# The first 8 MB load of a row-sum kernel, cut into four loads of 32 partitions that are four apart

## The chip, the cores and the metric

The kernel runs on one core of one Trainium2 chip. The metric is the device time of one execution in microseconds (us). Of the core's engines this kernel uses VectorE (DVE) and ScalarE (ACT) for arithmetic, SyncE (SP) to issue all transfers, and the core's 16 DMA engines to carry them out. GpSimd (POOL) only sets a few constants; TensorE does nothing.

## What is computed

```python
def setup_inputs():
    batch, seq, dim = 32, 512, 1024
    return {"x": np.random.randn(batch, seq, dim).astype(np.float32)}

def reference(x):
    relu_x = np.maximum(x, 0)
    return np.sum(relu_x, axis=-1).astype(np.float32)
```

There are 32 x 512 = 16,384 rows of 1,024 floats. Each is clamped at zero and summed. 67.1 MB are read, 64 KB are written.

## The kernel before

**Tiling.** The rows are split into two halves in name only: the first 2,048 rows (`xf`) and the rest (`xv`). In each, partition p holds consecutive rows, so that what one load brings to one partition is contiguous in memory. A full block is 16 rows for each of 128 partitions: 64 KB a partition, 8 MB in all. Three such buffers in on-chip memory (`io0`, `io1`, `io2`; `NBUF = 3`) are used in turn.

**Loop.** For each of seven blocks (`j`), `load` (L97) issues one transfer of 8 MB from SP into a buffer. From the fourth block on, it waits before that until DVE has read the buffer's former contents (`freed`). Each load has a semaphore of its own, which counts up by 16 as the transfer completes; the first computing instruction of the block waits for 16. In the first blocks ACT clamps the whole block in place (`clamp`, L115) and DVE then sums it along the rows (`total`, L123), in one, later two pieces a block (`TWO`). In the sixth and seventh blocks some rows are done by ACT alone (`act_row`, clamp and sum in one instruction) or by DVE alone (`dve_row`).

**Tail.** The last 8 MB come in loads that get smaller: 8 rows a partition, 4 rows, 2 rows and 280 elements (1,164 KB), 1 row and 260 elements (642 KB), and two pieces of 240 and 244 elements, so that little work is left after the last byte. ACT and DVE share these rows one by one. Three stores bring the sums out; the last waits for the very last sum.

**Order.** The order on every engine is the order in which the code names the instructions. All loads and stores are issued by SP on one queue, so they are carried out one behind the other. Nothing separates the engines at the start: `open_without_barrier` (L238) takes the drains and semaphore waits out of the opening block and moves SP's first `EARLY` loads (here one, L24, L48) from the body into the opening block, ahead of SP's first instruction there, so that they are issued before SP branches to the body. On SP the order is thus: the load of `io0`, the branch, the loads of `io1` and `io2`, then the loads that wait for DVE, the tail, the stores.

Of the kernel before, what the change touches and what calls it, by code (L numbers as in the profile page):

```python
# [9 lines left out]
ROWS = 16  # L10
NBUF = 3
# [9 lines left out]
START_PIECE, END_PIECE = 280, 260  # L21
PIECES = [240, 244]

EARLY = 1  # L24


def kernel(tc: tile.TileContext, x: bass.AP, out: bass.AP):
    nc = tc.nc
    sems = Semaphores(tc)

    tc.close()
    tc.compile()
    nc.cur_bb = nc.bb_map[tc.start_bb_name]
    body = nc.cur_bb.bb.instructions
    ends = list(body)
    body.clear()
    n_stores = relu_sum(nc, sems, x, out)
    body.extend(ends)


    nc.cur_bb = nc.bb_map[tc.start_bb_name + "_end"]
    nc.cur_bb.bb.instructions.clear()
    nums = sorted(s.num for s in (*sems.loads, sems.act, sems.dve))
    cleared = range(nums[0], nums[-1] + 1)
    assert len(cleared) == len(nums)
    nc.sync.sem_clear(cleared)
    nc.sync.wait_ge(sems.stored, 16 * n_stores).then_inc(sems.stored, -16 * n_stores)
    open_without_barrier(tc, EARLY)  # L48

# [10 lines left out]
def relu_sum(nc, sems: Semaphores, x: bass.AP, out: bass.AP):  # L60
    x_flat = x.flatten_outer_dims()
    N, D = x_flat.shape
    NT = N // P
    NB = len(TWO)
    assert N == P * NT == P * ROWS * (NB + 1)
    assert sum(TAIL) == ROWS - 4 and START_PIECE + END_PIECE + sum(PIECES) == D

    bufs = [nc.alloc_sbuf_tensor(f"io{i}", [P, ROWS, D], F32) for i in range(NBUF)]
    res = nc.alloc_sbuf_tensor("res", [P, NT], F32)

    extra = len(PIECES) + 1
    parts = [
        nc.alloc_sbuf_tensor(f"piece{i}", [P, w + extra * (i + 1 == len(PIECES))], F32)
        for i, w in enumerate(PIECES)
    ]


    N1 = P * ROWS
    xf = x_flat[:N1].rearrange("(p m) d -> p m d", p=P)
    xv = x_flat[N1:].rearrange("(p m) d -> p m d", p=P)  # L80
    o_flat = out.rearrange("b s -> (b s)")
    of = o_flat[:N1].rearrange("(p m) -> p m", p=P)
    ov = o_flat[N1:].rearrange("(p m) -> p m", p=P)

    def rows(m, n):
        if m < ROWS:
            return xf[:, m : m + n, :]
        return xv[:, m - ROWS : m - ROWS + n, :]

    def sums(m, n):  # L90
        if m < ROWS:
            return of[:, m : m + n], res[:, m : m + n]
        return ov[:, m - ROWS : m - ROWS + n], res[:, m : m + n]

    n_load = n_act = n_dve = n_store = 0

    def load(dst, src, after=None):  # L97
        nonlocal n_load
        dma = nc.sync.dma_start(out=dst, in_=src)  # L99
        if after:  # L100
            dma.wait_op(sems.dve, after[1], "sem-ge")
        dma.then_inc(sems.loads[n_load], 16)
        n_load += 1
        return sems.loads[n_load - 1]

    def store(m, n, act, dve):
        nonlocal n_store
        dst, src = sums(m, n)
        nc.sync.wait_ge(sems.act, act)
        nc.sync.dma_start(out=dst, in_=src).wait_op(sems.dve, dve, "sem-ge").then_inc(  # L110
            sems.stored, 16
        )
        n_store += 1

    def clamp(ap, loaded):  # L115
        nonlocal n_act
        i = nc.scalar.activation(out=ap, in_=ap, func=RELU)  # L117
        if loaded is not None:
            i.wait_op(loaded, 16, "sem-ge")
        i.then_inc(sems.act, 1)  # L120
        n_act += 1

    def total(ap, m, n):  # L123
        nonlocal n_dve
        nc.vector.tensor_reduce(  # L125
            out=res[:, m : m + n], in_=ap, axis=mybir.AxisListType.X, op=ADD
        ).wait_op(sems.act, n_act, "sem-ge").then_inc(sems.dve, 1)
        n_dve += 1

    def act_row(ap, accum_out, loaded):  # L130
        nonlocal n_act
        i = nc.scalar.activation(out=ap, in_=ap, func=RELU, accum_out=accum_out)  # L132
        if loaded is not None:
            i.wait_op(loaded, 16, "sem-ge")
        i.then_inc(sems.act, 1)
        n_act += 1

    def dve_row(ap, accum_out, loaded):
        nonlocal n_dve
        i = nc.vector.tensor_scalar(  # L140
            out=ap,
            in0=ap,
            scalar1=0.0,
            scalar2=None,
            op0=MAX,
            op1=ADD,
            accum_out=accum_out,
        )
        if loaded is not None:
            i.wait_op(loaded, 16, "sem-ge")  # L150
        i.then_inc(sems.dve, 1)
        n_dve += 1

    freed = []
    m = 0
    for j in range(NB):
        buf = bufs[j % NBUF]
        loaded = load(buf[:, :, :], rows(m, ROWS), j >= NBUF and freed[j - NBUF])
        c = 0
        act_waits = dve_waits = loaded  # L160
        for n in TWO[j]:
            clamp(buf[:, c : c + n, :], act_waits)
            total(buf[:, c : c + n, :], m + c, n)
            act_waits = None
            c += n
        for _ in range(ACT[j]):
            act_row(buf[:, c, :], res[:, m + c : m + c + 1], act_waits)
            act_waits = None
            c += 1
        for _ in range(DVE[j]):  # L170
            dve_row(buf[:, c, :], res[:, m + c : m + c + 1], dve_waits)
            dve_waits = None
            c += 1
        assert c == ROWS
        freed.append((n_act, n_dve))
        m += ROWS


    buf = bufs[NB % NBUF]
    c = 0  # L180
    for n in TAIL:
        loaded = load(
            buf[:, c : c + n, :], rows(m, n), None if c else freed[NB - NBUF]
        )
        for i in range(n):
            if i % 2 == 0 or (n == 8 and i == 7):
                act_row(buf[:, c, :], res[:, m : m + 1], loaded if i == 0 else None)
            else:
                dve_row(buf[:, c, :], res[:, m : m + 1], loaded if i == 1 else None)
            c += 1  # L190
            m += 1

    flat = buf[:, :, :].rearrange("p c d -> p (c d)")
    src = rows(m, 4).rearrange("p c d -> p (c d)")
    at = c * D
    split = 2 * D
    b = split + START_PIECE
    end = split + D - END_PIECE
    last, w = parts[-1], PIECES[-1]
    others = [last[:, w + i : w + i + 1] for i in range(extra)]  # L200
    loaded = load(flat[:, at : at + b], src[:, :b])
    act_row(buf[:, c, :], res[:, m : m + 1], loaded)
    sums_act = n_act
    dve_row(buf[:, c + 1, :], res[:, m + 1 : m + 2], loaded)
    sums_dve = n_dve
    dve_row(flat[:, at + split : at + b], others[0], None)
    loaded = load(flat[:, at + end : at + 4 * D], src[:, end:])
    act_row(buf[:, c + 3, :], res[:, m + 3 : m + 4], loaded)
    dve_row(flat[:, at + end : at + 3 * D], others[1], loaded)
    arrived = []  # L210
    for part, n in zip(parts, PIECES):
        arrived.append(load(part[:, :n], src[:, b : b + n]))
        b += n
    assert b == end

    store(0, ROWS, *freed[0])
    store(ROWS, NT - ROWS - 2, sums_act, sums_dve)

    for i in range(len(PIECES) - 1):
        dve_row(parts[i][:, :], others[2 + i], arrived[i])
    nc.vector.wait_ge(arrived[-1], 16)
    nc.vector.tensor_scalar(  # L224
        out=last[:, :],
        in0=last[:, :],
        scalar1=0.0,
        scalar2=None,
        op0=MAX,
        op1=ADD,  # L230
        accum_out=res[:, NT - 2 : NT - 1],
    ).wait_op(sems.dve, n_dve, "sem-ge").then_inc(sems.dve, 1)
    n_dve += 1
    store(NT - 2, 2, n_act, n_dve)
    return n_store


def open_without_barrier(tc: tile.TileContext, n_loads: int):  # L238

    SP = mybir.EngineType.SP
    blocks = tc.nc.main_func.blocks
    opening = blocks[0].instructions
    body = next(b for b in blocks if b.name == tc.start_bb_name).instructions
    for i in list(opening):
        if isinstance(i, (mybir.InstDrain, mybir.InstEventSemaphore)):
            opening.remove(i)
    loads = [i for i in body if i.engine == SP][:n_loads]
    for i in loads:  # L250
        assert isinstance(i, mybir.InstDMACopy)
        body.remove(i)
    at = next(n for n, i in enumerate(opening) if i.engine == SP)
    opening[at:at] = loads
# [30 lines left out]
```

## Time and profile before

| | |
|---|---|
| time, median of 3 runs | 161.14 us (161.03 to 161.29) |
| span of the profiled execution, first to last instruction | 159.62 us |
| busy: DVE | 117.6 us (74%) |
| busy: ACT | 104.2 us (65%) |
| DMA | 67.18 MB in 2,304 packets, mean 421 GB/s over the span |
| first load, issue to landing | 21.8 us |
| issue of the first load on SP | 0.38 us, from 0.00 |
| issues of the second and third load | 0.42 and 0.43 us, from 0.43 and 0.90 |

The profile is of one execution. It gives that execution's span; its device time was not taken beside it, so the median of the runs stands for it: 1.52 us more than the span, which lie before the first and after the last instruction.

Line numbers (L99) are lines of the kernel. "SPq" is SP's DMA queue as the issuer. A DMA packet here is one contiguous piece for one partition: 64 KB in the large loads. Its bytes are counted in the stretch of time in which the packet starts, so that GB/s over a short stretch is a count of packets that start in it. Arrows show who ended a wait.

### The profile page before, as it was taken

The numbers are of one execution on the slowest core, as the hardware profiler recorded it, in microseconds if no ns is written. First come the engines' busy times: TensorE is split into PE (matmuls) and PEld (weight loads), VectorE is DVE, ScalarE is ACT, GpSimd is POOL, SyncE is SP. The second block draws the span as 40 slices with busy tenths as digits, with TensorE's granted clock in tenths as the row PEclk, the third lists the DMA queues.
The fourth block names the chain that finished last, engine by engine and source line by source line (L and its number), as shares of the span: only waits on it lengthen the run. The fifth ranks groups of instructions, "written<-read, shape, count | busy, mean of one in ns | idle before, by whom it ended". The sixth has DMA issues, their size and how long they took to land.

```text
span 159.6 us, 120 instructions
## 1 busy us (share of the span) xinstructions
DVE 117.6 (74%) x43; ACT 104.2 (65%) x50; POOL 0.2 (0%) x4
## 2 busy tenths in 40 slices
DVE  0000000009999499994999999999999999999986
ACT  3000059990699708996099951999329993499995
POOL 0000000000000000000000000000000000000000
DMA  7996996996997999979979969969969969798993
GB/s 279 509 526 263 526 526 263 526 509 279 526 476 312 526 394 394 526 345 443 526 328 460 526 263 526 526 263 526 509 279 526 493 296 526 337 452 382 418 412 119
DMA packets 2304, 67.18 MB, mean 421 GB/s; under 512 B 640, under 2 KB 896, under 8 KB 1024
## 3 DMA queue, kind: packets, MB, share of 16 engines
q1 hardware_dynamic: 2304, 67.18, 98.0%
HBM read 67.11 MB, written 0.07 MB: 421 GB/s over the span
## 4 chain that ended last, share of the span: by engine, by line
DMA 43%; DVE 34%; ACT 17%; another core or an unknown queue 3%; SPq 1%; issue 0%
DMA io<-in_x_dram 43%; DVE res L125 32%; ACT io L117 17%; DVE io L140 1%; SPq L99 1%; DVE piece L224 0%; DVE piece L140 0%
## 5 line engine op out<-in xcount | busy, mean ns | idle before, releaser
L125 DVE TENSOR_REDUCE res<-io 128x8 f32<-128x8192 f32 (+2 forms) x9 | 101.1, 11287 | 40.0 <-ACT io L117 40.0
L117 ACT ACTIVATE io<-io 128x8192 f32<-128x8192 f32 (+2 forms) x9 | 81.7, 9110 | 47.7 <-DMA io<-in_x_dram 47.7
L132 ACT ACTIVATE io<-io 128x1024 f32<-128x1024 f32 x20 | 20.9, 1045 | 6.0 <-DMA io<-in_x_dram 6.0
L140 DVE TENSOR_SCALAR_CACHE_REDUCE io<-io 128x1024 f32<-128x1024 f32 (+2 forms) x15 | 15.8, 1110 | 0.5 <-DMA io<-in_x_dram 0.4
L132 ACT ACTIVATION_READ_ACCUMULATOR io<-io 128x1 f32 x20 | 3.8, 188 | 0.0
L117 ACT ACT_TABLE_LOAD x1 | 1.3, 1283 | 0.1
L140 DVE DVE_READ_ACCUMULATOR io<-io 128x1 f32 x15 | 1.2, 82 | 0.0
L224 DVE TENSOR_SCALAR_CACHE_REDUCE piece<-piece 128x247 f32<-128x247 f32 x1 | 0.4, 410 | 0.0
L140 DVE TENSOR_SCALAR_CACHE_REDUCE piece<-piece 128x240 f32<-128x240 f32 x1 | 0.4, 397 | 0.0
L269 POOL MEMSET const-bfloat16-1.0<- 128x1 bf16 x1 | 0.1, 101 | 0.0
L269 POOL MEMSET const-uint8-127<- 128x1 uint8 x1 | 0.1, 101 | 0.0
L269 POOL MEMSET const-float32-0.0<- 128x1 f32 x1 | 0.1, 98 | 0.2 <-issue 0.2
L269 POOL MEMSET const-float32-1.0<- 128x1 f32 x1 | 0.1, 98 | 0.0
L224 DVE DVE_READ_ACCUMULATOR piece<-piece 128x1 f32 x1 | 0.1, 83 | 0.0
L140 DVE DVE_READ_ACCUMULATOR piece<-piece 128x1 f32 x1 | 0.1, 82 | 0.0
## 6 DMA issues: line engine op xcount, KB each, us to landing
io<-in_x_dram SPq DMA_DIRECT2D x1, 4096.0 KB, 21.6
io<-in_x_dram SPq DMA_DIRECT2D x1, 2048.0 KB, 26.1
io<-in_x_dram SPq DMA_DIRECT2D x1, 1164.0 KB, 28.4
io<-in_x_dram SPq DMA_DIRECT2D x1, 642.0 KB, 29.5
piece<-in_x_dram SPq DMA_DIRECT2D x1, 122.0 KB, 29.2
piece<-in_x_dram SPq DMA_DIRECT2D x1, 120.0 KB, 29.4
io<-in_x_dram SPq DMA_DIRECT2D x7, 26.9
out_dram<-res SPq DMA_DIRECT2D x1, 55.0 KB, 1.6
```

Of the source, the lines that this page charges most:

```text
L99: dma = nc.sync.dma_start(out=dst, in_=src)
L117: i = nc.scalar.activation(out=ap, in_=ap, func=RELU)
L125: nc.vector.tensor_reduce(out=res[:, m : m + n], in_=ap, axis=mybir.AxisListType.X, op=ADD).wait_op(sems.act, n_act, "sem-ge").then_inc(se ...
L132: i = nc.scalar.activation(out=ap, in_=ap, func=RELU, accum_out=accum_out)
L140: i = nc.vector.tensor_scalar(out=ap, in0=ap, scalar1=0.0, scalar2=None, op0=MAX, op1=ADD, accum_out=accum_out,)
L224: nc.vector.tensor_scalar(out=last[:, :], in0=last[:, :], scalar1=0.0, scalar2=None, op0=MAX, op1=ADD, accum_out=res[:, NT - 2 : NT - 1],) ...
L269: nc = _bacc.Bacc("TRN2", target_bir_lowering=False, num_devices=1)
```

## The change

The first block's load is cut into four. Load q takes partitions q, q + 4, q + 8, ..., 32 of them, each with its whole 64 KB. The four are issued from SP one behind the other, count up the same semaphore by 16 each, and the first clamp waits for 64. `EARLY` is now 4, so all four go into the opening block, ahead of the branch. `load` returns the count to wait for beside the semaphore, and the helpers wait for that. On SP the order is now: four loads into `io0`, the branch, the loads of `io1` and `io2`, and all else as it was. No other engine's instructions change.

```diff
-EARLY = 1
+EARLY = 4
...
-        return sems.loads[n_load - 1]
+        return sems.loads[n_load - 1], 16
+
+    def load_in_parts(dst, src):
+        nonlocal n_load
+        for q in range(EARLY):
+            dma = nc.sync.dma_start(out=dst[q::EARLY], in_=src[q::EARLY])
+            dma.then_inc(sems.loads[n_load], 16)
+        n_load += 1
+        return sems.loads[n_load - 1], 16 * EARLY
...
-            i.wait_op(loaded, 16, "sem-ge")
+            i.wait_op(*loaded, "sem-ge")
...
-        loaded = load(buf[:, :, :], rows(m, ROWS), j >= NBUF and freed[j - NBUF])
+        if j == 0:
+            loaded = load_in_parts(buf[:, :, :], rows(m, ROWS))
+        else:
+            loaded = load(buf[:, :, :], rows(m, ROWS), j >= NBUF and freed[j - NBUF])
...
-    nc.vector.wait_ge(arrived[-1], 16)
+    nc.vector.wait_ge(*arrived[-1])
```

More of the change, by code (lines that the diff above doesn't have):

```diff
@@ L133, in act_row @@
         if loaded is not None:
-            i.wait_op(loaded, 16, "sem-ge")
+            i.wait_op(*loaded, "sem-ge")
         i.then_inc(sems.act, 1)
@@ L149, in dve_row @@
         if loaded is not None:
-            i.wait_op(loaded, 16, "sem-ge")
+            i.wait_op(*loaded, "sem-ge")
         i.then_inc(sems.dve, 1)
```

## The prediction

> **What bounds the kernel now.** I read the shares first. The page's DMA rows (mean busy share of the 16 engines in 40 slices, then the queue's total) and the span:
>
> ```profile
> span 159.6 us, 120 instructions
> ...
> DMA  7996996996997999979979969969969969798993
> ...
> q1 hardware_dynamic: 2304, 67.18, 98.0%
> ```
>
> The digits jump because a 64 KB packet is booked in the slice where it starts; the last line counts: the DMA engines were moving packets for 98% of the span. No compute engine comes near (DVE 74%, ACT 65%). Next, the order of time on ACT, whose clamps (L117) each wait for one whole 8 MB load:
>
> ```profile
> 21.87 13.86 ACT L117 ACTIVATE io<-io 128x16384 f32<-128x16384 f32 x1 [20.47 <-DMA io<-in_x_dram]
> 41.19 13.86 ACT L117 ACTIVATE io<-io 128x16384 f32<-128x16384 f32 x1 [5.46 <-DMA io<-in_x_dram]
> 60.55 13.86 ACT L117 ACTIVATE io<-io 128x16384 f32<-128x16384 f32 x1 [5.50 <-DMA io<-in_x_dram]
> 79.90 13.95 ACT L117 ACTIVATE io<-io 128x8192 f32<-128x8192 f32 x2 [5.50 <-DMA io<-in_x_dram]
> ```
>
> Columns: start, duration, instruction, idle before it and who ended that. Loads land 19.32 to 19.36 us apart. A load is 128 rows of 64 KB, 8 rows for each of 16 engines, so a row takes 19.35/8 = 2.42 us. The first load lands at 21.87, 2.5 us more than 19.35: that start-up is paid once, and since the queue never runs dry, a change of it shifts the end one for one. The queue's cover: io0 is issued again at 53.00, the queue has work until 60.5. At the end the chain of waits goes through a landing and then DVE alone:
>
> ```profile
> 126.91 28.43 DMA io<-in_x_dram
> 155.34 0.02 issue
> 155.37 2.02 DVE io L140 x6
> ```
>
> DVE had been idle 0.43 us before 155.37. Its earlier reduces start when ACT's clamps end, so they move with the landings too.
>
> Then the start-up in short windows (first column the window, second its width, last column GB/s; GB/s by width by 1/65,536 gives how many packets start there):
>
> ```profile
> 1.00:1.25 0.25, 0.00 (x0) 0.25 (x1) 0.00 (x0) 1.00 8.52 2884
> 1.25:1.50 0.25, 0.00 (x0) 0.15 (x1) 0.00 (x0) 1.00 1.47 524
> 1.50:1.75 0.25, 0.00 (x0) 0.00 (x0) 0.00 (x0) 1.00 1.41 524
> 1.75:2.00 0.25, 0.00 (x0) 0.00 (x0) 0.00 (x0) 1.00 0.62 262
> ...
> 3.95:4.20 0.25, 0.00 (x0) 0.00 (x0) 0.00 (x0) 1.00 3.02 1311
> 4.20:4.45 0.25, 0.00 (x0) 0.00 (x0) 0.00 (x0) 1.00 5.44 2359
> 4.45:4.70 0.25, 0.00 (x0) 0.00 (x0) 0.00 (x0) 1.00 1.21 524
> ```
>
> 11, 2, 2 and 1 engines start their first row in the first four; 5, 9 and 2 turn to their second row in the last three. Narrower windows put the first two turns between 3.90 and 4.00 and the last between 4.55 and 4.60: a spread of 0.6 us, with first rows that take about 3 us instead of 2.42. It stays: 130 us later (134.50 to 135.25) the counts by quarter microsecond are 6, 8 and 2. A load lands when its last engine is done, so the engine that turned at 4.58 sets every landing. What counts is that time.
>
> **The change, part by part.** Durations are from the execution whose span is 159.62 us; the median of the runs is 161.14, 1.52 more, which lies around the span and which nothing here touches. The sum is a difference, taken off both.
>
> *Removed and added.* One issue of 128 rows becomes four of 32, rows q, q+4, q+8 and so on. Same bytes, same 128 rows of 64 KB, all waited for together (count 64 instead of 16 on the same clamp). Four issues stand ahead of SP's branch where one did.
>
> *A, the last engine's turn.* If the spread of 0.62 comes from 128 rows being described to the engines in one go, a quarter of the rows leaves a quarter of it: a gain of 0.75 x 0.62 = 0.46. Against that stands the last store (L110): also 128 rows, but of 8 bytes, into an empty queue. Issued at 158.19, all its rows and completions pass between about 159.01 and 159.21, so its engines start at most about 0.15 us apart; three quarters of that is 0.11. The first load is nearer in size and place, the store cleaner; I take the middle, 0.29.
>
> *B, the first byte.* The first issue occupies SP for 0.38 us, the first packet starts at 1.01; the last store needs 0.82 from issue to first packet. If the issue shrinks with the rows, 0.75 x 0.38 = 0.29 is gained; if a 32-row issue costs what the later back-to-back ones do (0.42 to 0.46), 0.06 is lost. I take 0.13.
>
> *C, three more completions for each engine.* The last store is 9 packets on each engine (8 rows, 1 completion) in 0.2 us: at most 0.023 each, 0.07 for three. I take 0.03.
>
> *D, what is moved behind three more issues.* On SP the loads of io1 and io2 go out at about 1.8 and 2.2 instead of 0.43 and 0.90. They are needed when the first load's rows run out, at about 20.9: 18 us of cover. The re-issue of io0 at 53.00 waits for DVE (L125), not for SP. POOL's four sets and ACT's table load (over at 1.40) depend on none of it. Without that cover it would be 3 x 0.44 = 1.3 us. Cost 0.
>
> Sum: 0.29 + 0.13 - 0.03 = 0.39 gained, span 159.23, median 161.14 - 0.39 = 160.75. By the ends: 161.14 - 0.46 - 0.29 = 160.39, and 161.14 - 0.11 + 0.06 + 0.07 = 161.16.
>
> The row on splitting: loads queued behind each other land 19.35 us apart with no gap of their own. [...] No row here shows a 32-row load.
>
> **The rivals.**
>
> *R1, the spread is the memory's.* Each engine still opens with one 64 KB row, and its 3 us may come from the memory's first answers, whatever number of rows was described. For it: the last store's small spread, and that of the 16 engines the one starting last (after 1.75) isn't the one turning last, as 2.42 after 1.8 is below 4.58. Then A = B = 0, C 0.03: 161.17, no change that can be told. The change then does not do what it sets out to do.
>
> *R2, the run of issues holds the engines back (slower).* In the trace the engines' first starts, 1.0 to 1.8, fall in and just behind the time in which SP issues io1 and io2 (0.43 to 1.33). If each issue that follows takes the descriptions' path away from engines still to be started, the spread of 0.62 is 0.31 for each of two; now five follow, until about 2.6. Three more cost 0.93, C 0.03, against B's 0.13: 161.97. It decides as soon as the last engine turns after 4.58. Against it: 11 of 16 engines start by 1.25, with the third issue still under way.
>
> *R3, the rows are dealt badly (slower).* If 32 rows reach only 8 engines, or meet in pairs, the first load takes twice its 19.35: 161.14 + 19.35 = 180.5, hidden by nothing, since the queue is full. Against it: 32 is a multiple of 16, two rows for each; nothing in the trace speaks for it.
>
> **How the numbers follow.** My forecast, an earlier last engine, has 0.64; R1 0.13; R2 0.19; R3 0.04. A change under 0.2% (0.32 us) is about what a measurement of this kernel can't tell from none. The forecast's own range is 160.39 to 161.16; of its 0.64 I put 0.54 below 160.82 and 0.10 above. Faster 0.54; same 0.10 + 0.13 = 0.23; slower 0.19 + 0.04 = 0.23. The predicted time is 160.75. The range of 8 in 10 goes from 160.3, just past the best ends, up to 161.9, to the foot of R2's price; R3 and the upper part of R2 are left out.
>
> **What would show it.** A: the last engine's turn to its second row before 4.45, the counts by quarter microsecond bunched closer, and the same closeness 130 us on. B: first packets before 0.95. C: landings of the later loads still 19.35 apart. D: io1 issued near 1.8 with no dent in the DMA shares at 21. The first clamp should start near 21.5 instead of 21.87, and every later clamp as much earlier. R1 shows as an unchanged spread, R2 as first turns later than 4.6, R3 as a first clamp near 41. I am wrong if first rows keep their 3 us whatever the number described at once, or if DVE's 0.43 us of idle time before 155.37 closes, which would mean that something other than the landings has come to bind.

## The result and the profile after

| | before | changed |
|---|---|---|
| median of 8 runs each (lowest to highest) | 161.06 us (160.84 to 161.29) | 161.39 us (161.30 to 161.58) |
| ratio to before | | 1.002, 95% interval 1.0011 to 1.0029 |
| span of the profiled execution | 159.62 us | 160.00 us |
| first issue on SP | 0.38 us | 0.55 us |
| first clamp | 21.87 us | 22.22 us |

The change made the kernel 0.33 us slower, or 0.18 to 0.47 by the interval; the forecast was 0.39 us faster. The chain of waits of the changed kernel (start, duration, what) says where it begins:

```profile
0.00 0.55 SPq L109
0.55 0.06 issue
0.60 0.58 SPq L109
...
1.86 0.59 SPq L109
2.45 0.04 issue
2.49 39.06 DMA io<-in_x_dram
```

A 32-row part takes SP 0.55 to 0.59 us where the 128-row load took 0.38, and all four end at 2.45 instead of the 1.8 expected. The start-up in short windows (GB/s in the last column, to be read as a count of packets that start, as in the prediction):

```profile
1.00:1.25 0.25, 0.00 (x0) 0.25 (x1) 0.00 (x0) 1.00 0.00 0
1.25:1.50 0.25, 0.00 (x0) 0.15 (x1) 0.00 (x0) 1.00 6.40 2097
1.50:1.75 0.25, 0.00 (x0) 0.00 (x0) 0.00 (x0) 1.00 3.92 1311
...
4.20:4.45 0.25, 0.00 (x0) 0.00 (x0) 0.00 (x0) 1.00 1.82 786
4.45:4.70 0.25, 0.00 (x0) 0.00 (x0) 0.00 (x0) 1.00 3.63 1573
4.70:4.95 0.25, 0.00 (x0) 0.00 (x0) 0.00 (x0) 1.00 4.23 1835
```

Between 1.00 and 1.25, where 11 engines had started, none does; a narrower window puts the first starts between 1.30 and 1.35 instead of 1.01. The turns to the second row lie in the last three windows (3, 6 and 7 engines). The earliest falls between 4.30 and 4.35 instead of just before 4.00, the latest between 4.90 and 4.95 instead of 4.55 to 4.60. Both ends have moved by about 0.35; the spread is 0.6 as before. From there on the time only follows. ACT in order of time:

```profile
22.22 13.86 ACT L125 ACTIVATE io<-io 128x16384 f32<-128x16384 f32 x1 [20.83 <-DMA io<-in_x_dram]
41.58 13.86 ACT L125 ACTIVATE io<-io 128x16384 f32<-128x16384 f32 x1 [5.50 <-DMA io<-in_x_dram]
60.92 13.86 ACT L125 ACTIVATE io<-io 128x16384 f32<-128x16384 f32 x1 [5.49 <-DMA io<-in_x_dram]
```

The loads still land 19.34 to 19.36 us apart, each 0.35 to 0.4 later than before. Nothing is won back in the 140 us that follow, and nothing more is lost: from the first clamp to the end of the span it is 137.76 us before and 137.77 after.

So the question was which property of the new loads makes the first issue and the first packet late. Three theories: S, the step of four partitions from one row of a load to the next; N, the small number of rows in a load; Q, the run of further issues right behind the first one (the prediction's R2).

### The profile page after: what moved, and what is told of

It reads as the page before. It is cut to its first block, busy times and chain, and to the rows that moved or that the text cites. A ratio compares the mean times of both kernels' runs of the same rounds, so it can differ in the third digit from the quotient of the medians.

```text
span 160.0 us, 123 instructions
## 1 busy us (share of the span) xinstructions
DVE 117.6 (74%) x43; ACT 104.2 (65%) x50; POOL 0.2 (0%) x4
## 4 chain that ended last, share of the span: by engine, by line
DMA 42%; DVE 34%; ACT 17%; another core or an unknown queue 3%; SPq 2%; issue 0%
DMA io<-in_x_dram 42%; DVE res L133 32%; ACT io L125 17%; SPq L109 1%; DVE io L148 1%; SPq L99 0%; DVE piece L235 0%; DVE piece L148 0%
```

## The experiments

Unless a diff says otherwise, each kernel is the changed one with the edit shown. Times stand beside runs of the kernel before on the same chip: 161.03 us in the first set of four, 161.09 in the second, 161.11 in the third, 161.08 for the last run.

### Four loads of 32 neighbouring partitions

```diff
-            dma = nc.sync.dma_start(out=dst[q::EARLY], in_=src[q::EARLY])
+            near = slice(P // EARLY * q, P // EARLY * (q + 1))
+            dma = nc.sync.dma_start(out=dst[near], in_=src[near])
```

> The first 8 MB in four loads of 32 neighbouring partitions instead of partitions four apart; the output stays the reference's. Reference points: before, the first issue takes 0.38 us, the first packet starts at 1.01, the first clamp at 21.87; in the changed kernel 0.55, 1.33 and 22.22. Theory S (the step of four partitions makes a load's issue and start longer): issue near 0.38, first packet near 1.01. Theory N (few rows in a load do): 0.55 and 1.33 as in the change. Theory Q (the run of issues behind the first load holds its start back): 1.33 as in the change, the issue itself no judge. [...]

Measured: 181.90 us, ratio 1.1294 (1.1277 to 1.1310). SP's first issue, from its order of time, and the first window of starts:

```profile
0.00 0.38 SPq L110 DMA_DIRECT2D io<-in_x_dram  x1
```

```profile
0.95:1.20 0.25, 0.00 (x0) 0.25 (x1) 0.00 (x0) 1.00 11.05 2359
```

The issue takes 0.38 us again and nine engines have started by 1.20. The same window of the kernel before has ten:

```profile
0.95:1.20 0.25, 0.00 (x0) 0.25 (x1) 0.00 (x0) 1.00 7.75 2621
```

N falls: 32 rows cost SP no more than 128. The large loss is of another kind, as ACT shows:

```profile
43.02 13.86 ACT L126 ACTIVATE io<-io 128x16384 f32<-128x16384 f32 x1 [41.62 <-DMA io<-in_x_dram]
```

The first 8 MB need twice the time, which is the price that the prediction's R3 names. How the rows run, in windows of this kernel (the number before GB/s is the time of the packets that start in the window, as a share of 16 engines' time):

```profile
1.00:1.25 0.25, 0.00 (x0) 0.25 (x1) 0.00 (x0) 1.00 12.29 2621
1.25:2.00 0.75, 0.00 (x0) 0.15 (x1) 0.00 (x0) 1.00 2.23 524
2.00:4.00 2.00, 0.00 (x0) 0.00 (x0) 0.00 (x0) 1.00 0.00 0
...
8.00:12.00 4.00, 0.00 (x0) 0.00 (x0) 0.00 (x0) 1.00 1.28 262
```

Ten and six rows start by 2.00, so sixteen are under way, as in the kernel before, and not eight. But the 16 rows that start between 8 and 12 take 5.12 us each (1.28 x 16 x 4.00 us, shared by 16), where a row takes 2.42 in the kernel before and in the changed one. In these runs, then, 32 neighbours ran at about half rate and 32 partitions four apart at full rate; why, no view here shows.

### Two loads of 64 partitions, two apart

```diff
-EARLY = 4
+EARLY = 2
```

> The first 8 MB in two loads of 64 partitions that are two apart. S: as late as the change, issue near 0.55 and first packet near 1.33, since a step is there. N: between the two kernels, by rows about 1.22 (64 lies a third of the way from 32 to 128). Q: one more issue instead of three, a third of the change's delay, first packet near 1.12. Time above before by the same delay: S 0.32 us, N 0.2, Q 0.1.

Measured: 161.49 us, ratio 1.0029 (1.0018 to 1.0040). SP's first issue and the windows of the first starts:

```profile
0.00 0.54 SPq L109 DMA_DIRECT2D io<-in_x_dram  x1
```

```profile
1.20:1.30 0.10, 0.00 (x0) 0.10 (x1) 0.00 (x0) 1.00 0.00 0
1.30:1.50 0.20, 0.00 (x0) 0.10 (x1) 0.00 (x0) 1.00 10.94 3604
```

As long an issue and as late a start as with four loads of 32. Neither the number of rows (N) nor the number of issues behind (Q) grades the loss; that a step is there decides, as S has it.

### Four loads without a step: all partitions, four rows each

```diff
+            cut = slice(ROWS // EARLY * q, ROWS // EARLY * (q + 1))
-            dma = nc.sync.dma_start(out=dst[q::EARLY], in_=src[q::EARLY])
+            dma = nc.sync.dma_start(out=dst[:, cut], in_=src[:, cut])
```

> The first 8 MB in four loads of all 128 partitions, 4 of the 16 rows (16 KB a partition) each: as many issues as in the change, but no step in the partitions and no fewer of them. S and N: issue 0.38, first packet 1.01, time as before but for three more completions, +0.01 to +0.05 us. Q: first packet 1.33, time +0.3.

Measured: 161.00 us, ratio 0.9998 (0.9989 to 1.0008).

```profile
0.00 0.38 SPq L110 DMA_DIRECT2D io<-in_x_dram  x1
```

The first window of starts (its packets are 16 KB, so 524 GB/s are eight of them):

```profile
0.95:1.20 0.25, 0.00 (x0) 0.25 (x1) 0.00 (x0) 1.00 2.26 524
```

Its first clamp, in ACT's order of time:

```profile
21.80 13.86 ACT L126 ACTIVATE io<-io 128x16384 f32<-128x16384 f32 x1 [20.40 <-DMA io<-in_x_dram]
```

Four issues ahead of SP's branch, the wait for a count of 64 and three more completions for each engine cost nothing that can be measured: by the interval at most 0.13 us. Cutting the load was free here (161.00 us, ratio 0.9998); the way of cutting was not. Q falls: three issues stand right behind the first, and the first packets start by 1.20.

### The further issues held back

The first part goes out alone; parts two to four and the loads of `io1` and `io2` wait for an ACT instruction on a scratch tile, which is extra work. (The diff leaves out the new tile and two new semaphores.)

```diff
...
+    def hold():
+        nc.vector.memset(fill[:, :], 0.0).then_inc(sems.filled, 1)
+        nc.scalar.activation(out=fill[:, :], in_=fill[:, :], func=RELU).wait_op(
+            sems.filled, 1, "sem-ge"
+        ).then_inc(sems.go, 1)
+        nc.sync.wait_ge(sems.go, 1)
...
             dma.then_inc(sems.loads[n_load], 16)
+            if q == 0:
+                hold()
...
-    open_without_barrier(tc, EARLY)
+    open_without_barrier(tc, 1)
```

> The changed kernel, but SP issues parts two to four and the loads of io1 and io2 only after an ACT instruction that ends near 2.5 us (a scratch tile, filled by DVE and clamped by ACT, is extra work), when all 16 engines have begun their first row; the first part alone goes out in the opening block. Q: first packet back near 1.01, the last engine's turn near 4.6 or earlier, time at or below before. S and N: first issue 0.55, first packet 1.33, last turn 4.9, time as the change (+0.3). If the wait itself costs the later parts their cover, the second part's rows would start after the 6.7 at which the first part's end.

Measured: 161.47 us, ratio 1.0027 (1.0017 to 1.0037). The windows of the first starts:

```profile
0.95:1.20 0.25, 0.25 (x1) 0.25 (x1) 0.00 (x0) 1.00 0.00 0
1.20:1.30 0.10, 0.07 (x1) 0.10 (x1) 0.00 (x0) 1.00 0.00 0
1.30:1.50 0.20, 0.00 (x0) 0.19 (x2) 0.00 (x0) 1.00 10.95 3604
```

Its last engine's turn to the second row:

```profile
4.95:5.20 0.25, 0.00 (x0) 0.00 (x0) 0.00 (x0) 1.00 0.61 262
```

With SP silent behind the first part until 2.49, the first packet still starts after 1.30, and the last engine turns no sooner than in the change (after 4.95; there by 4.95). Q falls by this run alone, and with it the prediction's R2. The first clamp came at 22.32, with the loads after it 19.3 apart, so the held parts still had their cover.

### On which side of the transfer the step lies

```diff
+            near = slice(P // EARLY * q, P // EARLY * (q + 1))
-            dma = nc.sync.dma_start(out=dst[q::EARLY], in_=src[q::EARLY])
+            dma = nc.sync.dma_start(out=dst[q::EARLY], in_=src[near])
...
-    store(0, ROWS, *freed[0])
+    nc.sync.wait_ge(sems.act, freed[0][0])
+    nc.sync.wait_ge(sems.dve, freed[0][1])
+    for q in range(EARLY):
+        near = slice(P // EARLY * q, P // EARLY * (q + 1))
+        nc.sync.dma_start(out=of[near, 0:ROWS], in_=res[q::EARLY, 0:ROWS]).then_inc(
+            sems.stored, 16
+        )
+        n_store += 1
```

> Partitions four apart on chip as in the change, but each part reads 32 neighbouring 64 KB rows of memory (one stretch of 2 MB); the first block's sums are stored in four stores that put them in order again. If the step over on-chip partitions is what lengthens the first issue and the start: issue 0.55, first packet 1.33, time near 161.4. If the step between the rows in memory does it: issue 0.38, first packet 1.01, time near 161.0.

The second kernel of the pair has `out=dst[near], in_=src[q::EARLY]` in the load, and the store turned round in the same way.

> The other way round: each part reads rows of memory four apart and puts them into 32 neighbouring partitions; stores in four parts too. If the on-chip step is the cause: issue 0.38, first packet 1.01. If the memory's step is: 0.55 and 1.33. [...]

Measured: 161.73 us, ratio 1.0038 (1.0025 to 1.0051), with the step on chip; 182.10 us, ratio 1.1307 (1.1293 to 1.1322), with the step in memory. Step on chip, SP's first issue and the windows:

```profile
0.00 0.58 SPq L110 DMA_DIRECT2D io<-in_x_dram  x1
```

```profile
1.20:1.30 0.10, 0.00 (x0) 0.10 (x1) 0.00 (x0) 1.00 0.00 0
1.30:1.50 0.20, 0.00 (x0) 0.10 (x1) 0.00 (x0) 1.00 8.80 2621
```

Step in memory, the same two views:

```profile
0.00 0.39 SPq L110 DMA_DIRECT2D io<-in_x_dram  x1
```

```profile
0.95:1.20 0.25, 0.00 (x0) 0.25 (x1) 0.00 (x0) 1.00 14.27 3146
```

Only the step over on-chip partitions made the issue long (0.58 us against 0.39) and the start late. Twelve engines have started by 1.20 where the step is in memory alone. That kernel loses about as much as the four loads of 32 neighbours (182.10 us, there 181.90), and like them it fills neighbouring on-chip partitions; with the step on chip alone no such loss appears. The kernel with the step on chip alone lost 0.64 us against before on its chip, about twice what the change lost and 0.3 more than expected. In its profile the first clamp comes at 22.61: one engine starts its first row only after 2.60, the first rows took 3.4 us on average instead of the change's 3.1, and the last turn to a second row comes after 5.25. This second half of its loss is not the longer issue's; that it reads neighbouring stretches of memory may be the reason, which no run here shows.

### The same four loads where the queue has work

```diff
-        if j == 0:
+        if j == 1:
...
-    open_without_barrier(tc, EARLY)
+    open_without_barrier(tc, 1)
```

> The same four loads of 32 partitions four apart, but for the second block (io1), behind a whole first load whose rows keep the queue busy until 20.9 us. If the on-chip step costs time only between the issue and the first packet of an empty queue: first issue 0.38, first packet 1.01, the second clamp still about 19.33 after the first, time as before (within 0.1 us). If stepped loads also move their rows slower or leave gaps: the second clamp later by that, time up to 0.3 above before.

Measured: 161.03 us, ratio 1.0000 (0.9991 to 1.0008).

```profile
22.19 13.86 ACT L125 ACTIVATE io<-io 128x16384 f32<-128x16384 f32 x1 [20.79 <-DMA io<-in_x_dram]
41.52 13.86 ACT L125 ACTIVATE io<-io 128x16384 f32<-128x16384 f32 x1 [5.47 <-DMA io<-in_x_dram]
```

The stepped block lands 19.33 us after the block before it, and the time is that of before. The first stepped issue takes 0.53 us here too, but the queue has the first load to move meanwhile. In these runs the longer issue cost time only where the queue was empty. (The profiled execution took 161.29 us, 0.26 more than the median, and its first clamp is late; the distance of the two is what counts.)

### A start with small packets

Cut by rows of a partition instead of by partitions, all 128 in each load. The number of rows in the first load varies.

```diff
-EARLY = 4
+EARLY = 2
+CUTS = [0, 4, ROWS]
...
+            cut = slice(CUTS[q], CUTS[q + 1])
-            dma = nc.sync.dma_start(out=dst[q::EARLY], in_=src[q::EARLY])
+            dma = nc.sync.dma_start(out=dst[:, cut], in_=src[:, cut])
```

Eight loads of 2 rows each (`EARLY = 8` in the kernel of four loads without a step) came first, then the version in the diff, 4 rows and 12, twice:

> Eight loads of all 128 partitions, 2 rows (8 KB a partition) each. With four such loads the 16 engines' completions of the first block lay 0.31 us apart instead of 0.62 and the first clamp came 0.07 earlier. If smaller first packets draw the engines together further: spread near 0.15, first clamp near 21.7, time 0.1 below before. If four was enough or each added load costs its own few hundredths: spread 0.3, time 160.95 to 161.1.

> Two loads of all 128 partitions, 4 rows then 12: only the first packets are small (16 KB). If it is the small first packets that draw the engines together: spread near 0.3 and first clamp near 21.8 as with four loads, time at 160.95 to 161.05. If the rest must be small as well: spread 0.6, time as before.

> The kernel with two loads of all partitions (4 rows, then 12) once more, for a narrower interval. If the bunched engines are worth what the first clamp showed (0.12 us earlier): time 0.1 to 0.15 below before again. If the 0.17 of the first comparison was chance: within 0.05 of before.

2 rows and 14 (`CUTS = [0, 2, ROWS]`), 1 row and 15 (`CUTS = [0, 1, ROWS]`):

> Two loads of all partitions, 2 rows (8 KB a partition), then 14. If smaller first packets start the stream sooner: first clamp near 21.7 and time 0.1 to 0.2 below before. If 14-row packets of 56 KB spread the engines again: spread 0.6 and time as before.

> Two loads of all 128 partitions, 1 row (4 KB a partition), then 15. The first clamp came at 21.87 with one load, 21.69 to 21.75 with 4 rows first and 21.58 with 2 rows first. If the small first packet sets it: 21.5 or earlier and a time 0.2 to 0.35 below before. If the 0.5 MB of the first part (1.2 us of all engines) is too little to cover the second load's start: a gap behind the first packets, first clamp later than 21.6 and time between that of 2 rows first and before.

| loads of the first block | time, us | ratio to before (95%) | first clamp | engines' completions apart |
|---|---|---|---|---|
| one (before) | 161.03 to 161.11 | 1 | 21.87 | 0.62 |
| 4 x 4 rows | 161.00 | 0.9998 (0.9989 to 1.0008) | 21.80 | 0.31 |
| 8 x 2 rows | 161.16 | 1.0004 (0.9996 to 1.0013) | 22.08 | 0.51 |
| 4, 12 rows | 160.92 | 0.9994 (0.9985 to 1.0002) | 21.75 | 0.38 |
| 4, 12 rows again | 160.97 | 0.9991 (0.9982 to 1.0000) | 21.69 | 0.37 |
| 2, 14 rows | 160.83 | 0.9984 (0.9975 to 0.9992) | 21.58 | 0.57 |
| 1, 15 rows | 161.29 | 1.0016 (1.0007 to 1.0025) | 22.24 | 0.56 |

The last two columns are of one profiled execution each; the last is the time in us from the first to the last of the 16 engines' completions of the first block, read from the trace's packets. Smaller first packets don't always bunch the engines, and the bunching isn't what gains: the fastest of these kernels has its completions about as far apart as before.

Two rows first, then fourteen, is faster than before by 0.28 us in the medians, and so beats both kernels; it is the best of five ways of cutting and was not run a second time. Its first two clamps:

```profile
21.58 13.86 ACT L127 ACTIVATE io<-io 128x16384 f32<-128x16384 f32 x1 [20.18 <-DMA io<-in_x_dram]
40.92 13.86 ACT L127 ACTIVATE io<-io 128x16384 f32<-128x16384 f32 x1 [5.49 <-DMA io<-in_x_dram]
```

Both are 0.27 to 0.29 earlier than before, as much as the medians differ, which points to a gain at the start. The profiled execution itself didn't keep it: it took 161.04 us, with a span of 159.70, and in the tail DVE's row behind the 1,164 KB load started at 155.27, only 0.10 earlier than before, and the one behind the 642 KB load at 157.03, 0.08 later. So the gain rests on the runs, and that it is at the start is likely, not shown. With one row first it turns into a loss; part of it shows in the windows of that kernel:

```profile
1.75:2.00 0.25, 0.00 (x0) 0.00 (x0) 0.00 (x0) 1.00 0.77 262
2.00:2.25 0.25, 0.00 (x0) 0.00 (x0) 0.00 (x0) 1.00 0.87 344
2.25:2.50 0.25, 0.00 (x0) 0.00 (x0) 0.00 (x0) 1.00 0.99 410
2.50:2.75 0.25, 0.00 (x0) 0.00 (x0) 0.00 (x0) 1.00 2.20 918
```

From 1.75 to 2.50 the engines move only 262 to 410 GB/s in 4 KB packets, below the 434 of the steady stream (8.39 MB in 19.35 us), and the large rows start only after 2.5. In its trace these 60 KB packets then take 2.33 us on average, where the stream's rate gives 2.27; with two rows first, the 56 KB packets take 2.12, as in the stream. Why they differ isn't shown. Eight small loads didn't help either. Smaller was thus not always better; two rows are the best of what was tried, and I have no theory that gives this number.

## Why the prediction was wrong

*What bounds the kernel* was right: a queue that is never empty, so that a change of the start moves the end one for one. First packet +0.32, last engine's turn +0.35, first clamp +0.36, span +0.37 (from unrounded times), medians +0.33. DVE's idle time before the tail's last rows stayed open, at 0.42 us. The 1.52 us that the prediction set around the span are about 0.17 too many if the profile before is like all later ones, which have their own time: there it is 1.34 to 1.36. The forecast difference doesn't rest on it.

*Two terms of the sum failed*, B more than A. The forecast was a first clamp 0.39 earlier, and it came 0.36 later. Of these 0.75 us B has 0.45 (0.13 gained in the sum, 0.32 lost) and A 0.32 (0.29 gained in the sum, 0.03 lost); C took 0.02 less than its 0.03.

*B, the first byte, is the step that failed by its sign.* The prediction took the issue to shrink with the rows, or at worst to cost what the back-to-back issues do, and put 0.13 us of gain between bounds of -0.06 and 0.29. Measured: 0.32 lost. The number of rows played no part (32 neighbours: 0.38 us, start by 1.20). The step over partitions, which no load of the kernel before has, did it all: 0.54 to 0.58 us of issue and a start after 1.30 in each of the four kernels whose first load has it, 0.37 to 0.39 and a start near 1.0 in each kernel without. The bounds came from rows that differ from the new load in size alone, while its new property was the access pattern; a loss outside these bounds should have been left open.

*A, the last engine's turn*, was to gain 0.29 if the spread came from the number of rows described in one go, which was an assumption: no view shows the describing. The spread stayed at 0.6 with a quarter of the rows in the first issue, and with the others held back, and the first rows kept their 3 us, which is the prediction's own sign of being wrong. Among the profiles whose first 8 MB come at full rate the completions of the first block lie from 0.31 us apart (four loads of 4 rows) to 0.9 (stepped loads in the second block). The last store's small spread, the evidence that I weighed lower, was the better guide, and R1 had this half right. What does set the spread stays open.

*C, three more completions*: 0.03 expected. The first clamp moved by 0.01 more than the last turn, and the four loads without a step cost nothing measurable.

*D, the moved loads*, was right in its cost of 0: `io1` went out at 2.49 and `io2` at 3.12 instead of 1.8 and 2.2, and the 18 us of cover hid it.

*The rivals.* R2 named the right sign and, with 161.97, a size too large, and its mark, last turns after 4.6, appeared; but its mechanism is not there: holding the later issues back didn't help. R3 doesn't hold for partitions four apart, whose rows took 2.42 us as before. Its price holds for neighbours, which cost 20.9 us against its 19.35, though with sixteen rows under way and not eight. The measured 161.39 lies inside the stated range, on a side that had 0.23; as that side was there for R2 and R3, this is luck. The prediction also held that a change under 0.2% can't be told from none: here 0.2% stood clear of the interval's half-width of 0.09%.

*What stays open.* SP's first issue grows by 0.17 us and the first packet is 0.32 late. That both go with the on-chip step is shown, why the issue is longer with it is not; where the other 0.15 us is spent, between the end of the issue and the first packet, no view shows.

## What to carry to other kernels

Where one queue carries everything, look at the first load: its longer issue cost 0.33 us here, and the same step in the second block's load cost nothing (161.03 us, ratio 1.0000). So give the first load an access pattern without a step on chip, and take a step over on-chip partitions where the queue already has work. Look at what is new in an instruction's form, not only in its size, before bounding its cost by its neighbours' rows. If the first load is to be cut, cut along the partition's own data and measure: over all partitions a first part of two rows gained 0.16% here and one of one row lost as much, while a cut by partitions lost 0.2 to 0.4% with a step and 13% without.

## What was unexpected of the hardware

In the first load an on-chip step of two or four partitions made the issue 0.16 to 0.20 us longer than the 0.38 of before and the first packet 0.31 to 0.36 us later than 1.01, with 32 rows and with 64. Behind other issues the difference is less clear: in the first 6 us of all runs these took SP 0.47 to 0.60 us with a step and 0.41 to 0.59 without. And the first packet of each engine was slow in all four sizes that were run, as read from the packets of the traces. A 64 KB row that took 2.42 us in the stream took about 3 at the start; 16 KB took about 1.1 us (0.60 by the stream's rate), 8 KB about 0.5 (0.30) and 4 KB 0.27 (0.15).
